# Residual additions, the fourth block difference and two operand splits on VectorE instead of GpSimd, in a two-layer hybrid trunk

## The chip, the cores and the metric

The kernel runs on one core of a Trainium2 chip. The metric is the time of one execution on the device in microseconds (us). The engines go by the profile's names: PE is TensorE (its matmuls), PEld TensorE's weight loads, DVE VectorE, ACT ScalarE, POOL GpSimd, and SP the queue that issues the DMA transfers. Each engine works through a queue of its own in order and waits on semaphores for the others. TensorE's clock is shown as a share of 2.4 GHz, so that 0.50 is its lower level of 1.2 GHz.

## What is computed

An input of 1024 rows by 1024 features goes through two layers, all in float32. In each layer a mixer and a SwiGLU channel mixer (FFN) sit inside a pair of norms with a residual addition:

```python
def rmsnorm(x, g):
    y = x * lax.rsqrt(jnp.mean(x * x, axis=-1, keepdims=True) + RMS_EPS)
    return y * g

def sandwich(x, g_pre, g_post, fn):
    return x + rmsnorm(fn(rmsnorm(x, g_pre)), g_post)

def swiglu(h, w_gate, w_up, w_down):
    return (jax.nn.silu(h @ w_gate) * (h @ w_up)) @ w_down

def even_mixer(t, ...):          # layer 0
    proj = t @ w_in
    y_a = diff_attention(proj[..., :3 * DIFF_WIDTH], ...)
    y_b = conformer_conv(proj[..., 3 * DIFF_WIDTH:], ...)
    return jnp.concatenate([y_a, y_b], axis=-1) @ w_out

def odd_mixer(t, ...):           # layer 1
    proj = t @ w_in
    y_c = s5_ssm(proj[..., :o1], ...)
    y_d = mla_attention(...)
    return jnp.concatenate([y_c, y_d], axis=-1) @ w_out

for layer in (0, 1):
    h = sandwich(h, mix_pre, mix_post, mixer)
    h = sandwich(h, ffn_pre, ffn_post, swiglu)
```

The FFN's inner width is 2816. The state-space layer (s5) needs a few dozen small preparations of its coefficients (exponentials, sines, quotients), each on 128 x 8 numbers.

## The kernel before

**Products.** Each float32 operand of a product is split into a high part (a rounded copy, made by ACT) and a low part (operand minus high part, made by DVE or POOL). A product is then three matmuls (`mm3`, L118 to L120): high by high, high by low, low by high. For the weights of the FFN this is `wsplit`: ACT casts `wh` (L1119), POOL subtracts `wl` (L1121).

**The output projection and its norm.** `w_out_last` runs over eight blocks of 128 rows, once in layer 0 (about 440 to 540 us) and once in layer 1 (about 1610 to 1720 us). Per block it loads a partial sum `pa`, splits the mixer's output into `jt` (high part by ACT L484, low part by DVE L485; one buffer), multiplies it with 4 units of weights in two column halves (24 matmuls into `psw`), and adds each half to `pa` on DVE (L510). Then `sandwich` takes over: the sum of squares on ACT (L106), `rstd` on POOL (L97, L98), the scaling with the post-norm on DVE (L164), the residual addition `nr <- nr + pa` (L165) on the engine that the caller names, a store of `nr`, a second sum of squares and the scaling with the pre-norm on DVE (L169). `nr` has two buffers, `pa` three.

**Into the FFN.** Two blocks later, `Ffn.to_T` transposes the normalised block on TensorE (eight transposes into PSUM `tr`) and cuts it into quarter blocks: `B11`, `B21`, `B22` as high and low parts (L1087, L1088), and four sums or differences kept in `F0` and `F1` (L1080, L1083, L1090, L1091, L1092). The FFN's up projection then follows a one-level fast scheme with seven products instead of eight for each pair of column blocks. `pre` makes the first two products (`b1`, `b2`) of the first pairs between the last blocks of the loop: `c = p + b2` on DVE (L1161) frees the PSUM of `b2`. `x_sums` splits the differences into `T1` to `T4` (L1099 high parts on ACT, L1100 low parts). `pair` makes the products `b5`, `b6`, `b3`, `b7`, `b4` of the differences of weights (`raw`, L1170 and L1171 on DVE) with `T2`, `B22` and so on, and adds them into `p` and `F` on DVE (L1170). `b4` takes the PSUM buffers ("tr") of `b5`, which `F <- p + b5` frees. In layer 0 the small preparations of the state-space layer (`s5_prep`, L525 to L716) lie in the same stretch.

**Order.** The order of the instructions on each engine is not the program's. A scheduler of the framework sorts them, working from its own simulated times; so when an operation is given to another engine, the rows around it, and some far from it, may be sorted otherwise.

Of the kernel before, what the change touches and what calls it, by code (L numbers as in the profile page):

```python
# [10 lines left out]
F32 = mybir.dt.float32  # L11
F32R = mybir.dt.float32r
# [8 lines left out]
P = 128  # L21
S = 1024
D = 1024
HALF = 512
# [11 lines left out]
class Trunk:  # L36
# [134 lines left out]
    def to_T(self, xn, X, b):  # L171
        nc = self.nc
        for q in range(2):
            tr = self.pp.tile([P, 4, P], F32, tag="tr", name="tr")
            for k in range(4):
                d = q * 4 + k
                nc.tensor.transpose(tr[:, k, :], xn[:, d * P:(d + 1) * P], self.ident)
            hi = X[q][:, :, 0, b * P:(b + 1) * P]
            nc.scalar.copy(hi, tr)
            nc.vector.tensor_tensor(X[q][:, :, 1, b * P:(b + 1) * P], tr, hi.bitcast(F32), op=ALU.subtract)  # L180
# [321 lines left out]
    def w_out_last(self, Y, src, res, hout, gpost, gpre, G, pool, fin=None):  # L502
        nc = self.nc
        units = [self.unit(s) for s in src]
        done = []
        for tb in range(8):
            a = pool.tile([P, D], F32, tag="pa", name="pa", bufs=3)
            nc.sync.dma_start(a, self.part[tb * P:(tb + 1) * P, :])
            for cs, ps in self.w_out(Y, units, tb, pool, self.ob, 1):
                nc.vector.tensor_tensor(a[:, cs], ps, a[:, cs], op=ALU.add)  # L510
            self.sandwich(a, tb, res, hout, gpost, gpre, pool.tile([P, D], F32, tag="nr", name="nr", bufs=2), nc.gpsimd)
            done.append(a)
            if tb == 0 and fin is not None:
                fin()
            if tb >= 2:
                G.to_T(done[tb - 2], tb - 2)
            if tb == 6:
                G.pre(0, 0)
        G.pre(0, 1)
        G.to_T(done[6], 6)  # L520
        G.pre(1, 0)
        G.to_T(done[7], 7)
        G.pre(1, 1)
# [528 lines left out]
class Ffn:  # L1052
# [15 lines left out]
    def to_T(self, xn, tb):  # L1068
        K, nc = self.K, self.nc
        t, b = tb // 4, tb % 4  # L1070
        bs = slice(b * P, (b + 1) * P)
        v, sub = nc.vector.tensor_tensor, ALU.subtract
        f0, f1 = [[F[:, q, :, bs] for q in range(2)] for F in (self.F0, self.F1)]
        for q in range(2):
            tr = K.pp.tile([P, 4, P], F32, tag="tr", name="tr")
            for k in range(4):
                d = q * 4 + k
                nc.tensor.transpose(tr[:, k, :], xn[:, d * P:(d + 1) * P], K.ident)
            if t == 0:
                nc.scalar.copy(f0[q], tr)  # L1080
            elif q == 0:
                nc.scalar.copy(f1[0], tr)
                v(f0[0], tr, f0[0], op=sub)  # L1083
            if (q, t) in self.B:
                B = self.B[q, t]
                hi = B[:, :, 0, bs]
                nc.scalar.copy(hi, tr)  # L1087
                v(B[:, :, 1, bs], tr, hi.bitcast(F32), op=sub)  # L1088
        if t:
            v(f1[1], tr, f0[0], op=sub)  # L1090
            v(f1[0], tr, f1[0], op=sub)  # L1091
            nc.gpsimd.tensor_tensor(f0[1], f0[1], f1[1], op=sub)  # L1092

    def x_sums(self, pool):
        nc, K = self.nc, self.K
        F0, F1 = self.F0, self.F1

        def split(T, src, eng):
            nc.scalar.copy(T[:, :, 0, :], src)  # L1099
            eng.tensor_tensor(T[:, :, 1, :], src, T[:, :, 0, :].bitcast(F32), op=ALU.subtract)  # L1100
            return T

        t = lambda n: pool.tile([P, 4, 2, HALF], F32R, tag="tc", name=n, bufs=2)
        self.T1 = split(K.yp.tile([P, 4, 2, HALF], F32R, tag="y", name="T1"), F0[:, 0], nc.vector)
        self.T2 = split(t("T2"), F1[:, 1], nc.vector)
        self.T3 = split(t("T3"), F1[:, 0], nc.gpsimd)
        self.T4 = split(self.bx.tile([P, 4, 2, HALF], F32R, tag="f", name="T4"), F0[:, 1], nc.gpsimd)
        self.E = F0.rearrange("p q (k d) c -> p (q k) d c", d=2)

    def raw(self, src, n=2):  # L1110
# [440 lines left out]
```

## Time and profile before

| | |
|---|---|
| time, median of 3 runs | 2391.94 us (2391.46 to 2400.63) |
| the profiled execution | 2392.32 us, its span 2390.5 us |
| mean granted clock of TensorE | 0.955 |
| TensorE busy | 2172.1 us (91% of the span) |
| VectorE busy | 1587.8 us (66%) |
| ScalarE busy | 952.2 us (40%) |
| GpSimd busy | 1393.1 us (58%) |

"Busy" adds up the time in which an engine has an instruction under way. That includes time in which the instruction is held up by another engine, so a mean duration far above the shortest of the same kind is itself a finding. The chain of work that ended last, which the profile follows back from the end, covers only the last part of the span here; for the stretches around the change the waits of TensorE by line and the timelines are read.

### The profile page before, as it was taken

The numbers are of one execution on the slowest core, as the hardware profiler recorded it, in microseconds if no ns is written. First come the engines' busy times: TensorE is split into PE (matmuls) and PEld (weight loads), VectorE is DVE, ScalarE is ACT, GpSimd is POOL, SyncE is SP. The second block draws the span as 40 slices with busy tenths as digits, with TensorE's granted clock in tenths as the row PEclk, the third lists the DMA queues.
The fourth block names the chain that finished last, engine by engine and source line by source line (L and its number), as shares of the span: only waits on it lengthen the run. The fifth ranks groups of instructions, "written<-read, shape, count | busy, mean of one in ns | idle before, by whom it ended". The sixth has DMA issues, their size and how long they took to land. (4 is left out here: it accounts for less than half of the span.)

```text
span 2390.5 us, 27147 instructions
## 1 busy us (share of the span) xinstructions
PE 2172.1 (91%) x9684; PEld 1755.7 (73%) x9684; DVE 1587.8 (66%) x2091; ACT 952.2 (40%) x1419; POOL 1393.1 (58%) x790
## 2 busy tenths in 40 slices
PE   7999889876999999899768888998799999999995
PEld 5887677665888878688656776876688888877874
DVE  6869567679756865677883467756764444448778
ACT  5554555442222232433243346654522222234332
POOL 5997202264665556787843536423775656569786
PEclk9999899988999999999888999999899999999997
DMA  5134663342332333655453375324432323255543
GB/s 206 62 120 146 172 175 102 107 149 69 121 115 97 125 129 106 198 161 163 125 178 104 110 234 154 115 80 148 138 102 93 127 72 132 75 177 163 164 130 132
DMA packets 153735, 315.34 MB, mean 132 GB/s; under 512 B 20224, under 2 KB 43904, under 8 KB 153600
## 3 DMA queue, kind: packets, MB, share of 16 engines
q1 hardware_dynamic: 153600, 313.60, 40.8%
q8 instruction: 77, 1.26, 0.2%
q14 instruction: 58, 0.48, 0.1%
HBM read 214.39 MB, written 96.01 MB: 130 GB/s over the span
## 5 line engine op out<-in xcount | busy, mean ns | idle before, releaser
L1121 POOL TENSOR_TENSOR wl<-raw,wh 128x1024 fp32r<-128x1024 f32 (+1 forms) x238 | 607.4, 2556 | 335.9 <-ACT wh L1119 319.4
L1119 ACT CAST wh<-raw 128x1024 fp32r<-128x1024 f32 (+1 forms) x238 | 242.7, 1023 | 456.8 <-PE b L119 258.9
L118 PE MATMUL b<-T,wh 128*128 128x512 f32 x704 | 277.9, 396 | 16.3 <-DVE F L1170 13.0
L120 PE MATMUL b<-T,wl 128*128 128x512 f32 x704 | 277.4, 394 | 1.1 <-POOL wl L1121 1.1
L119 PE MATMUL b<-T,wh 128*128 128x512 f32 x704 | 277.7, 394 | 0.6 <-DVE T L1100 0.6
L118 PE MATMUL psd<-wh,hh 128*128 128x512 f32 x552 | 222.8, 404 | 37.7 <-DVE acc L1229 26.5
L118 PE MATMUL b<-B,wh 128*128 128x512 f32 x528 | 209.2, 397 | 21.2 <-DVE c L1161 17.6
L119 PE MATMUL psd<-wl,hh 128*128 128x512 f32 x552 | 219.9, 398 | 0.0
L120 PE MATMUL psd<-wh,hl 128*128 128x512 f32 x552 | 219.1, 398 | 0.0
L119 PE MATMUL b<-B,wh 128*128 128x512 f32 x528 | 208.2, 395 | 0.7 <-DVE B L1088 0.7
L120 PE MATMUL b<-B,wl 128*128 128x512 f32 x528 | 207.7, 395 | 0.8 <-POOL wl L1121 0.8
L1229 DVE TENSOR_TENSOR acc<-acc,psd 128x1024 f32<-128x1024 f32 x124 | 150.7, 1217 | 82.7 <-PE psd L120 82.6
L1170 DVE TENSOR_TENSOR p<-p,b 128x1024 f32<-128x1024 f32 (+1 forms) x88 | 83.4, 949 | 144.6 <-PE b L120 134.7
L1248 ACT CAST hh<-hr 128x1024 fp32r<-128x1024 f32 (+1 forms) x84 | 82.4, 981 | 240.0 <-PE psd L119 215.1
L118 PEld LDWEIGHTS b<-T,wh 128*128 128x128 f32 x704 | 133.1, 189 | 47.8 <-issue 13.6
L118 PEld LDWEIGHTS psd<-wh,hh 128*128 128x128 f32 x552 | 106.1, 192 | 70.1 <-issue 27.9
L91 POOL TENSOR_TENSOR wl<-raw,wh 128x1024 fp32r<-128x1024 f32 x48 | 121.6, 2546 | 61.6 <-ACT wh L89 61.4
L120 PEld LDWEIGHTS b<-T,wl 128*128 128x128 f32 x704 | 133.1, 189 | 31.8 <-POOL wl L1121 1.5
L119 PEld LDWEIGHTS b<-T,wh 128*128 128x128 f32 x704 | 133.3, 189 | 31.0 <-DVE T L1100 1.1
L1249 DVE TENSOR_TENSOR hl<-hr,hh 128x1024 fp32r<-128x1024 f32 (+1 forms) x84 | 145.7, 1738 | 11.9 <-ACT hh L1248 11.9
L1273 POOL TENSOR_TENSOR raw<-raw 128x1024 f32<-128x1024 f32 (+1 forms) x50 | 123.4, 2468 | 20.7 <-DMA raw<-in_l_dn_dram 18.3
L1171 DVE TENSOR_TENSOR raw<-raw 128x1024 f32<-128x1024 f32 x66 | 108.3, 1640 | 40.4 <-POOL wl L1121 39.1
(420 smaller groups left out, 5209.2 us busy)
## 6 DMA issues: line engine op xcount, KB each, us to landing
raw<-in_l_gu_dram SPq DMA_DIRECT2D x96, 512.0 KB, 3.5
hr<-l_h_s SPq DMA_DIRECT2D x70, 512.0 KB, 3.9
raw<-in_l_dn_dram SPq DMA_DIRECT2D x48, 512.0 KB, 3.8
l_h_s<-F SPq DMA_DIRECT2D x66, 256.0 KB, 2.2
raw<-in_w_in_dram SPq DMA_DIRECT2D x27, 512.0 KB, 4.0
l_h_s<-c SPq DMA_DIRECT2D x44, 256.0 KB, 2.0
l_h_s<-p SPq DMA_DIRECT2D x44, 256.0 KB, 2.4
raw<-in_l_w_out_dram SPq DMA_DIRECT2D x16, 512.0 KB, 4.1
```

Source lines behind the costliest of these rows:

```text
L91: nc.gpsimd.tensor_tensor(lo, raw, hi.bitcast(F32), op=ALU.subtract)
L118: mm(ps, ah, bh, start=first, stop=False)
L119: mm(ps, ah, bl, start=False, stop=False)
L120: mm(ps, al, bh, start=False, stop=last)
L1119: nc.scalar.copy(hi[:, 0:n], r[:, 0:n])
L1121: nc.gpsimd.tensor_tensor(lo[:, 0:n], r[:, 0:n], hi[:, 0:n].bitcast(F32), op=ALU.subtract)
L1170: add = lambda o, a, b: v.tensor_tensor(o, a, b, op=ALU.add)
L1171: sub = lambda o, a, b: v.tensor_tensor(o, a, b, op=ALU.subtract)
L1229: add = lambda o, a, b: v.tensor_tensor(o, a, b, op=ALU.add)
L1248: nc.scalar.copy(hi[:, 0:n], r[:, 0:n])
L1249: v.tensor_tensor(lo[:, 0:n], r[:, 0:n], hi[:, 0:n].bitcast(F32), op=ALU.subtract)
L1273: g = lambda o, x, y: nc.gpsimd.tensor_tensor(o[:, s], x[:, s], y[:, s], op=ALU.subtract)
```

## The change

Three edits give operations from POOL to DVE. The residual additions of `w_out_last` (L165, 16 of 128x1024, eight per layer) go to DVE; the additions at the end of the FFNs (which have other callers) stay where they are. The fourth block difference in `to_T` (L1092, 8 of 128x512) goes to DVE. The low parts of `T3` and `T4` in `x_sums` (L1100, 4 of 128x2048, two per layer) go to DVE.

```diff
@@ w_out_last
             for cs, ps in self.w_out(Y, units, tb, pool, self.ob, 1):
                 nc.vector.tensor_tensor(a[:, cs], ps, a[:, cs], op=ALU.add)
-            self.sandwich(a, tb, res, hout, gpost, gpre, pool.tile([P, D], F32, tag="nr", name="nr", bufs=2), nc.gpsimd)
+            self.sandwich(a, tb, res, hout, gpost, gpre, pool.tile([P, D], F32, tag="nr", name="nr", bufs=2), nc.vector)
             done.append(a)
@@ Ffn.to_T
             v(f1[1], tr, f0[0], op=sub)
             v(f1[0], tr, f1[0], op=sub)
-            nc.gpsimd.tensor_tensor(f0[1], f0[1], f1[1], op=sub)
+            v(f0[1], f0[1], f1[1], op=sub)
@@ Ffn.x_sums
         self.T1 = split(K.yp.tile([P, 4, 2, HALF], F32R, tag="y", name="T1"), F0[:, 0], nc.vector)
         self.T2 = split(t("T2"), F1[:, 1], nc.vector)
-        self.T3 = split(t("T3"), F1[:, 0], nc.gpsimd)
-        self.T4 = split(self.bx.tile([P, 4, 2, HALF], F32R, tag="f", name="T4"), F0[:, 1], nc.gpsimd)
+        self.T3 = split(t("T3"), F1[:, 0], nc.vector)
+        self.T4 = split(self.bx.tile([P, 4, 2, HALF], F32R, tag="f", name="T4"), F0[:, 1], nc.vector)
```

The scheduler sorts the queues anew. Three places are shown, all on DVE; the number behind a name is that of its buffer.

The first is one block of the loop in layer 0: the block whose sum is `pa_4136` and whose split is `jt_4205`. Before:

```order
L510 TENSOR_TENSOR pa_4136<-psw_4141,pa_4136 128x512
L169 SCALAR_TENSOR_TENSOR pa_4002<-nr_4035,rstd_4049,gpre_3874 128x1024
L164 SCALAR_TENSOR_TENSOR pa_4069<-pa_4069,rstd_4107,gpost_3872 128x1024
L510 TENSOR_TENSOR pa_4136<-psw_4155,pa_4136 128x512
L485 TENSOR_TENSOR jt_4205<-yattn_2337,jt_4205 128x4x128
L1088 TENSOR_TENSOR B11_3864<-tr_4187,B11_3864 128x4x128
L1088 TENSOR_TENSOR B21_3865<-tr_4195,B21_3865 128x4x128
```

Now:

```order
L510 TENSOR_TENSOR pa_4136<-psw_4141,pa_4136 128x512
L510 TENSOR_TENSOR pa_4136<-psw_4155,pa_4136 128x512
L169 SCALAR_TENSOR_TENSOR pa_4069<-nr_4102,rstd_4116,gpre_3874 128x1024
L485 TENSOR_TENSOR jt_4205<-yattn_2337,jt_4205 128x4x128
L164 SCALAR_TENSOR_TENSOR pa_4136<-pa_4136,rstd_4174,gpost_3872 128x1024
L1088 TENSOR_TENSOR B11_3864<-tr_4254,B11_3864 128x4x128
L165 TENSOR_TENSOR nr_4169<-nr_4169,pa_4136 128x1024
L1088 TENSOR_TENSOR B21_3865<-tr_4262,B21_3865 128x4x128
```

The residual addition L165 stands between the two `B` splits. The two norm scalings have moved by a block: L164 now belongs to the block whose projection has just ended (`pa_4136`, before it was the one ahead of it), L169 to the block ahead of that, and the transposed block comes one block earlier.

The second is the tail of the loop in layer 0: `c11` are the sums that free `b2`, `raw` the weight sums of the first pair. Before:

```order
L1170 TENSOR_TENSOR raw_4612<-raw_4608,raw_4610 128x1024
L1171 TENSOR_TENSOR raw_4608<-raw_4604,raw_4608 128x1024
L169 SCALAR_TENSOR_TENSOR pa_4270<-nr_4303,rstd_4317,gpre_3874 128x1024
L164 SCALAR_TENSOR_TENSOR pa_4371<-pa_4371,rstd_4409,gpost_3872 128x1024
L1171 TENSOR_TENSOR raw_4612<-raw_4612,raw_4604 128x1024
L1083 TENSOR_TENSOR F0_3868<-tr_4478,F0_3868 128x4x128
L1088 TENSOR_TENSOR B22_3866<-tr_4485,B22_3866 128x4x128
L1171 TENSOR_TENSOR raw_4606<-raw_4606,raw_4612 128x1024
L1090 TENSOR_TENSOR F1_3867<-tr_4485,F0_3868 128x4x128
L1091 TENSOR_TENSOR F1_3867<-tr_4485,F1_3867 128x4x128
L1161 TENSOR_TENSOR c11_4471<-p1_4369,b2_4445 128x512
L1161 TENSOR_TENSOR c11_4472<-p1_4369,b2_4446 128x512
```

Now:

```order
L169 SCALAR_TENSOR_TENSOR pa_4270<-nr_4303,rstd_4317,gpre_3874 128x1024
L1170 TENSOR_TENSOR raw_4612<-raw_4608,raw_4610 128x1024
L164 SCALAR_TENSOR_TENSOR pa_4371<-pa_4371,rstd_4409,gpost_3872 128x1024
L1171 TENSOR_TENSOR raw_4608<-raw_4604,raw_4608 128x1024
L165 TENSOR_TENSOR nr_4404<-nr_4404,pa_4371 128x1024
L1171 TENSOR_TENSOR raw_4612<-raw_4612,raw_4604 128x1024
L1161 TENSOR_TENSOR c11_4471<-p1_4369,b2_4445 128x512
L1161 TENSOR_TENSOR c11_4472<-p1_4369,b2_4446 128x512
```

The residual addition of the last block stands ahead of `c11`; the quarter-block operations of the block before (L1083 to L1091) and one weight difference (`raw_4606`) now stand behind it.

The third is the start of the pairs in layer 0. Before, the low parts of `T1` and `T2` are followed by 97 rows, nearly all of them small ones of `s5_prep` (`xd` is one of its tiles), and only then by the additions of the first pair. Its first rows before:

```order
L1100 TENSOR_TENSOR T1_4592<-F0_3868,T1_4592 128x4x512
L544 TENSOR_SCALAR xd1_5313<-xd1_5313 128x8
L1100 TENSOR_TENSOR T2_4595<-F1_3867,T2_4595 128x4x512
L545 SCALAR_TENSOR_TENSOR xd2_5314<-xd1_5313,xd0_5312 128x8
L546 SCALAR_TENSOR_TENSOR xd2_5314<-xd1_5313,xd2_5314 128x8
L547 TENSOR_SCALAR xd3_5315<-xd2_5314 128x8
```

Now `T3` follows `T2` after one small row, `T4` after eight more, and the additions of the pair begin seven rows behind `T4`:

```order
L1100 TENSOR_TENSOR T4_4601<-F0_3868,T4_4601 128x4x512
L593 COPY dt_5311<-xd3_5315 128x8
L596 TENSOR_TENSOR x_5438<-lam_5303,dt_5311 128x8
L542 TENSOR_SCALAR xm0_5441<-x_5438 128x8
L543 TENSOR_SCALAR xm1_5442<-xm0_5441 128x8
L601 TENSOR_SCALAR x_5438<-x_5438 128x8
L544 TENSOR_SCALAR xm1_5442<-xm1_5442 128x8
L1170 TENSOR_TENSOR raw_4798<-raw_4794,raw_4796 128x1024
L545 SCALAR_TENSOR_TENSOR xm2_5443<-xm1_5442,xm0_5441 128x8
L1170 TENSOR_TENSOR p1_4369<-p1_4369,b6_4645 128x1024
L1171 TENSOR_TENSOR raw_4794<-raw_4790,raw_4794 128x1024
```

The addition `F0 <- p1 + b5`, on which `b4` waits, stands three rows further on, and some 80 small rows that stood ahead of it now stand behind it, among the pairs that follow.

## Rows read from the trace of the kernel before

**Rows 1.** The page's first part: busy us of each engine (share of span) xinstructions.

```profile
PE 2172.1 (91%) x9684; PEld 1755.7 (73%) x9684; DVE 1587.8 (66%) x2091; ACT 952.2 (40%) x1419; POOL 1393.1 (58%) x790
```

**Rows 2.** Waits of PE, 440 to 620 us: line, releaser: us in total, times, longest.

```profile
PE b L118 <- DVE F L1170: 13.0, 1, 13.0
PE b L118 <- DVE c L1161: 8.5, 1, 8.5
PE psw L120 <- DVE jt L485: 3.6, 3, 1.7
PE psw L118 <- ACT jt L484: 3.0, 3, 1.4
PE b L118 <- ACT wh L1119: 2.5, 1, 2.5
```

**Rows 3.** Waits of PE, 1610 to 1790 us.

```profile
PE b L118 <- DVE c L1161: 9.1, 1, 9.1
PE psw L120 <- DVE jt L485: 5.1, 4, 1.7
```

**Rows 4.** POOL's groups (busy us, mean ns), then DVE's by line (ns min/median/max, starts).

```profile
L165 POOL TENSOR_TENSOR nr<-nr,pa 128x1024 f32<-128x1024 f32 x16 | 40.0, 2501 | 39.1 <-DVE pa L164 37.7 <-PE psw L120 1.5
L1100 POOL TENSOR_TENSOR T<-F,T 128x2048 fp32r<-128x2048 f32 x4 | 20.7, 5163 | 10.9 <-ACT T L1099 10.9
L1092 POOL TENSOR_TENSOR F<-F,F 128x512 f32<-128x512 f32 x8 | 10.8, 1351 | 1.1 <-DVE F L1090 0.8
...
L165 DVE TENSOR_TENSOR acc<-acc,acc x12: 1207/1224/2771, 1209.6 to 2385.1; 128x1024 f32<-128x1024 f32 x12
...
L1100 DVE TENSOR_TENSOR T<-F,T x4: 2273/2276/2279, 552.0 to 1738.5; 128x2048 fp32r<-128x2048 f32 x4
```

**Rows 5.** Timeline, block loop, layer 0 (start us, us; [idle before]); last, all of L485.

```profile
482.93 1.28 DVE L164 SCALAR_TENSOR_TENSOR pa<-pa,rstd,gpost 128x1024 f32<-128x1024 f32 x1
...
484.72 2.49 DVE L485 TENSOR_TENSOR jt<-yattn,jt 128x512 fp32r<-128x512 f32 x1
...
484.28 2.38 POOL L165 TENSOR_TENSOR nr<-nr,pa 128x1024 f32<-128x1024 f32 x1 [3.26 <-DVE pa L164]
...
487.26 0.51 PE L120 MATMUL psw<-wh,jt 128*128 128x512 f32 x1 [1.67 <-DVE jt L485]
...
L485 DVE TENSOR_TENSOR jt<-yattn,jt x16: 683/1834/2508, 447.1 to 1681.8; 128x512 fp32r<-128x512 f32 x16
```

**Rows 6.** Stretches: length, busy us (instructions) by engine, then PE's clock, DMA share, GB/s.

```profile
487.30:491.00 3.70, 3.70 (x10) 2.91 (x11) 1.11 (x2) 1.59 (x4) 1.47 (x4) 0.55 0.45 175
584.40:589.60 5.20, 5.20 (x12) 4.09 (x13) 5.20 (x7) 0.36 (x1) 2.54 (x1) 0.50 0.00 0
600.00:620.00 20.00, 20.00 (x88) 16.23 (x87) 19.86 (x16) 4.73 (x5) 13.25 (x7) 0.99 0.54 165
```

**Rows 7.** Timelines of DVE and of POOL, tail of the loop in layer 0.

```profile
528.98 3.37 DVE L164 SCALAR_TENSOR_TENSOR pa<-pa,rstd,gpost 128x1024 f32<-128x1024 f32 x1
...
534.61 2.18 DVE L1171 TENSOR_TENSOR raw<-raw 128x1024 f32<-128x1024 f32 x1
...
532.43 3.27 POOL L165 TENSOR_TENSOR nr<-nr,pa 128x1024 f32<-128x1024 f32 x1 [1.16 <-DVE pa L164]
535.66 3.34 POOL L1121 TENSOR_TENSOR wl<-raw,wh 128x1024 fp32r<-128x1024 f32 x1
```

**Rows 8.** Timeline of DVE, T stage of layer 0, 556 to 585 us.

```profile
556.47 4.64 DVE L545 SCALAR_TENSOR_TENSOR xd<-xd,xd 128x8 f32<-128x8 f32 x1
561.15 2.33 DVE L546 SCALAR_TENSOR_TENSOR xd<-xd,xd 128x8 f32<-128x8 f32 x1
563.52 4.53 DVE L547 TENSOR_SCALAR xd<-xd 128x8 f32<-128x8 f32 x1
...
572.93 0.16 DVE L570 TENSOR_TENSOR cs<-cs 128x8 f32<-128x8 f32 x1
...
583.55 1.27 DVE L1170 TENSOR_TENSOR F<-p,b 128x512 f32<-128x512 f32 x2
...
```

## Prediction, made before the changed kernel was run

> **What bounds the kernel now.** I read the page first, then TensorE's waits, then the timelines around the longest of them. The page's busy line says TensorE (PE) is busy for 91% of the span, with VectorE (DVE) at 1587.8 us and GpSimd (POOL) at 1393.1 us [rows 1]. So a change on DVE and POOL is worth only what it takes from TensorE's idle stretches and from the slow clock behind them. Nearly all code that the diff touches lies in two stretches: the output projection of layer 0 and the start of its FFN (about 440 to 620 us), and the same in layer 1 (about 1610 to 1790 us). In the first, TensorE loses 13.0 us to the wait for `F` (L1170), 8.5 us to `c` (L1161), 3.6 us in three pieces to `jt` (L485) and 3.0 us in three to ACT's half of `jt`; 2.5 us go to a cast of `wh` [rows 2]. In the second, `c` costs 9.1 us and `jt` 5.1 us in four pieces; no wait for `F` stands there [rows 3]. From 600 us on TensorE is busy in all 20 us of a 20 us window [rows 6], so time won before that point is not handed to another wait at once.
>
> Each of these waits has the same pattern behind it. In the block loop POOL begins an addition `nr` at 484.28 us; DVE's lo half of `jt`, which starts 0.44 us later, takes 2.49 us where the shortest of the same line takes 0.683 us, and TensorE idles 1.67 us for it [rows 5]. So a DVE operation that reads two operands and starts while a POOL addition runs ends about when that addition does. In the tail of the loop, L164 takes 3.37 us and L1171 2.18 us in the same way, where undisturbed ones take 1.28 and some 1.22 us [rows 4, 5, 7]; both stand ahead of the `c` additions that TensorE waits for. In the T stage three operations on 128x8 elements take 4.64, 2.33 and 4.53 us, where one of their kind takes 0.16 us [rows 8]; POOL's two T splits of layer 0 run beside them, at 5.16 us each on average [rows 4].
>
> A wait also costs clock. Behind the wait at 487 us ten matmuls fill 3.70 us at a granted clock of 0.55, and behind the one at 584 us twelve fill 5.20 us at 0.50, against 88 in 20.00 us at 0.99 [rows 6]. At 20.00/88 = 0.227 us a matmul, this is 1.4 and 2.5 us lost beside the idle time itself.
>
> **The change part by part.**
>
> Work that moves. POOL loses 16 additions of 2.50 us (40 us), 8 of 1.35 us (11 us) and 4 splits of 5.16 us (21 us). DVE gains 16 at 1.22 us (19.6 us, by the additions of the same shape that it already does), 8 at about half of that (an estimate, half as wide: 4.9 us) and 4 at 2.27 us (9.1 us) [rows 4]. POOL's 72 us and DVE's 34 us lie beside other work, so their sums cost nothing by themselves; what counts is the place in the queue.
>
> (1) The block loops. The row of `nr` moves into DVE's queue, behind L485 and L164 of its block as the order shows, so L485 can no longer be held by it. The 3.6 us of layer 0 go, and at least the one slow stretch of 1.4 us: 5.0 us. In layer 1 I take the 5.1 us of four waits and no clock: 5 us. The cover is DVE's own time: a block holds 24 matmuls, 24 x 0.227 = 5.4 us, and eight transposes, and DVE's seven operations in it are, by the nearest rows, two 128x1024 scalings of 1.28 us, one addition of 1.22 us and four 128x512 of about 0.68 us [rows 4, 5, 7], 6.5 us in sum. That is tight: what is late next is ACT's half of `jt` (3.0 us stay in the sum) or DVE itself. Ends: nothing (if L485 stands behind L169 and L164 for as long as it was held), or 3.6 + 5.1 + 7 x 1.4 = 18 us. I take 10, since one slow stretch of three is on a row.
>
> (2) The tails, `c` in each layer. DVE's L164 comes down from 3.37 us to some 1.28 (2.1 us), and L1171 from 2.18 us to 1.22 (1.0 us); the addition itself, 1.22 us, now stands ahead of `c` on DVE. Net 1.9 us. POOL, free of an addition of 3.27 us and of a fourth difference of 1.35 us, can make the next `wl` earlier [rows 4, 7]: at most 4.6 us more. So between a loss of 1 us (nothing held any longer than now, the addition added) and a gain of 6 us; I take 4 in each layer, 8 in all. What is late next is the same `c`, some 4 us.
>
> (3) The T stage of layer 0. From the end of T2's split (556.5 us) to the `F` additions (583.55 us) DVE takes 27 us, of which 11.5 are the three held operations and the rest 94 small ones of the state-space preparation [rows 8]. In the new order T3 and T4 (2 x 2.27 = 4.5 us), some 16 small ones (2.6 us) and three additions of 1.22 us stand there: 10.8 us, so `F` could be freed at about 567 us. TensorE ran out of work 13.0 us before the wait's end at 584.4, at 571.4 [rows 2, 6]. By that the whole 13.0 us go; I take 10, leaving room for one or two holds of 2 us by POOL's `wl` that still run there. With the wait goes the slow stretch, 2.5 us [rows 6], and the wait for `wh` (2.5 us [rows 2]), whose `raw` sum stands in the same DVE queue. Sum 15 us. Ends: 5 us (if three holds of about 2 us and the small operations stay ahead) and 18 us. In layer 1 no TensorE wait for `F` is on the page, and T3 and T4 there are worth nothing.
>
> (4) The rest. The final additions of layer 1 stay with POOL; the rest of the program is only re-sorted by a few rows, and I count it at nothing, within 5 us either way, more than the 2.5 us of the `wh` wait and less than the sum of two such.
>
> By the profile the shared hold works both ways: a POOL addition of 2.50 us becomes a DVE one of 1.22 us, which can hold POOL for half as long [rows 4]. The Trainium skill speaks against the change here: *Perfetto Trace Analysis*, section "Optimizing Scalar/DVE Operations", says that GpSimd and DVE share an SBUF read port, so that moving operations between the two might not help. By that sentence nothing would be gained and the time would stay near 2392 us; the trace agrees on the sharing, but shows DVE to be twice as fast at the same operation.
>
> **The rivals.**
>
> - *Everything comes in.* 18 + 11 + 18 = 47 us: 2345 us. For it: each hold is on a row and its cause leaves the queue. Against: POOL's `wl` (3.34 us in the tail [rows 7]) goes on holding DVE.
> - *Only the loops gain.* In the tails and the T stage DVE's longer queue takes the place of the holds: the additions, T3 and T4 are 1.22 and 2 x 2.27 us of in-order work ahead of `c` and `F`, and `wl` still blocks. Then 10 us remain: 2382 us. This is where the shared-port argument would lead as a mechanism of this kernel. For it: DVE is busy for 19.86 of 20 us right behind the stage [rows 6]. Against: TensorE's 13.0 us of idle time is more than the 4.5 us that are added.
> - *DVE becomes the bound of the first FFN pairs: slower.* The order puts some 80 small state-space operations behind the `F` additions, among the pairs that follow, where TensorE has no idle time. They are 80 x 0.16 = 13 us undisturbed; one in four held for 2 us, as L164 is [rows 7], makes 40 us more. With DVE at 19.86 of 20 us [rows 6], they would be TensorE's wait: 2392 - 33 + 53 = 2412 us. It decides from 45 us of such waits on (2404 - 2359). Against: DVE has room in later pairs, and only what frees a PSUM buffer stops TensorE.
>
> **How the numbers follow.** The profiled execution took 2392.32 us against a median of 2391.94, so the sum stands for both. 10 + 8 + 15 = 33 us less: 2359 us, between 2347 and 2375 by the ends of the terms taken singly. Chances: forecast 0.59, everything 0.18, only the loops 0.15, slower 0.08. A measurement of this kernel tells about 0.5% (12 us) from no change, so the bounds are 2380 and 2404. Faster takes the first two, and a third of the third: 0.81; same is the rest of the third and the near side of the last: 0.12; slower 0.07. The range goes from 2340 (everything, and 5 us of re-sorting) to 2382.
>
> **What would show it.** Right: the `jt` waits of L485 near zero and its median near 0.69 us; `c` waits of about 4 us; the `F` wait under 3 us, with no stretch at half clock behind it; about 28 more DVE operations and POOL's busy time down by some 70 us. The first rival shows L164 or L165 on DVE held by `wl` and the `F` wait still above 8 us. The slower one shows new waits of TensorE for L1170 between 600 and 700 us behind rows of 128x8. I am wrong if TensorE's waits in the two stretches go and the span doesn't shorten: then the gain was given back in a part that I count at nothing.

## The result

The changed kernel takes 2360.12 us (median of 4 runs, 2357.66 to 2364.36) against 2391.7 us (median of 4 runs, 2388.27 to 2400.63) for the kernel before: a ratio of 0.986, with a 95% interval of 0.9835 to 0.9886, or 32 us. The forecast was 2359 us, within 2340 to 2382.

The first lines of the page after, which answer to [rows 1] (busy us, share of the span, instructions):

```profile
span 2359.2 us, 27146 instructions
...
PE 2167.2 (92%) x9684; PEld 1751.7 (74%) x9684; DVE 1598.5 (68%) x2119; ACT 953.0 (40%) x1419; POOL 1329.8 (56%) x762
```

DVE has 28 operations more and is busy for only 10.7 us more, though [rows 4] price what it took over at 34 us: by that difference some 23 us of its busy time before was time in which POOL held it (an estimate, net of the new holds shown below). POOL is busy 63 us less, not the 72 us that it gave away, since its other operations take a little longer now (`wl` 2.68 us on average, before 2.63).

TensorE's waits after, first in layer 0 (440 to 640 us), then in layer 1 (1590 to 1770 us); line, releaser: us in total, times, longest. They answer to [rows 2, 3]:

```profile
PE b L118 <- DVE c L1161: 4.0, 1, 4.0
PE b L120 <- POOL wl L1121: 3.9, 2, 3.5
PE psw L118 <- ACT jt L484: 3.5, 5, 1.3
PE b L118 <- DVE F L1170: 1.7, 1, 1.7
PE psw L118 <- DVE pa L510: 1.5, 2, 0.8
...
PE b L118 <- DVE c L1161: 4.5, 1, 4.5
PE psw L118 <- ACT jt L484: 3.2, 3, 1.3
PE b L118 <- ACT B L1087: 3.1, 1, 3.1
PE b L119 <- DVE B L1088: 2.3, 1, 2.3
PE b L118 <- DVE pa L510: 1.9, 1, 1.9
```

The waits for L485 are gone from both stretches, `F` is down from 13.0 to 1.7 us, `c` from 8.5 and 9.1 to 4.0 and 4.5. New or longer are the waits for `wl` (3.5 us) in layer 0, for `B` (3.1 and 2.3 us) in layer 1, and for DVE's additions L510 (1.5 and 1.9 us), which now stand behind others in its queue.

L485 in the two loops and the lines moved (ns min/median/max, first and last start), and three stretches (length, busy us of PE, PEld, DVE, ACT, POOL, then PE's clock, DMA share, GB/s). They answer to [rows 4 to 6]:

```profile
L485 DVE TENSOR_TENSOR jt<-yattn,jt x16: 678/685/693, 448.1 to 1649.8; 128x512 fp32r<-128x512 f32 x16
L165 DVE TENSOR_TENSOR nr<-nr,pa x16: 1209/1215/3384, 459.0 to 1675.8; 128x1024 f32<-128x1024 f32 x16
L1092 DVE TENSOR_TENSOR F<-F,F x8: 673/691/2274, 508.1 to 1694.8; 128x512 f32<-128x512 f32 x8
L1100 DVE TENSOR_TENSOR T<-F,T x8: 2272/2275/2292, 540.7 to 1705.1; 128x2048 fp32r<-128x2048 f32 x8
...
487.30:491.00 3.70, 3.70 (x21) 3.16 (x21) 3.00 (x4) 2.06 (x4) 0.94 (x2) 1.00 0.74 219
563.90:569.00 5.10, 5.08 (x23) 4.24 (x23) 5.10 (x12) 1.69 (x2) 1.45 (x1) 1.00 0.29 84
601.80:607.60 5.80, 5.76 (x14) 4.50 (x15) 5.80 (x8) 0.00 (x0) 3.35 (x2) 0.50 0.11 36
```

L485 is never held in the two loops (0.69 us at most). The moved operations take what was forecast at their median, and can be held themselves: L165 for 3.38 us at worst, L1092 for 2.27. The first two stretches run at full clock; the third, behind the new wait for `wl`, at half clock.

**Where the time went** is read best from one and the same matmul in both traces. The table gives its start before and after, and what was won or lost since the row above (the shift is after minus before):

| event on TensorE | before | after | shift | since the row above |
|---|---|---|---|---|
| first matmul of the projection's last part, layer 0 | 447.12 | 448.13 | +1.0 | |
| its last matmul (end of the loop) | 515.44 | 510.55 | -4.9 | -5.9 loop |
| first product with a `T` (end of the tail) | 554.56 | 545.41 | -9.2 | -4.3 tail |
| 337th FFN matmul into `b` | 625.64 | 597.62 | -28.0 | -18.9 T stage |
| 481st FFN matmul into `b` | 658.62 | 637.92 | -20.7 | +7.3 given back |
| first matmul of the down projection | 985.25 | 964.84 | -20.4 | +0.3 |
| its last, layer 0 | 1197.14 | 1174.51 | -22.6 | -2.2 |
| first matmul of the scan, layer 1 | 1318.52 | 1291.94 | -26.6 | -4.0 |
| last product of the attention, layer 1 | 1624.61 | 1597.66 | -27.0 | -0.4 |
| last matmul of the projection, layer 1 | 1691.86 | 1659.13 | -32.7 | -5.8 loop |
| first product with a `T`, layer 1 | 1734.02 | 1701.71 | -32.3 | +0.4 tail |
| last matmul of the program | 2378.84 | 2347.54 | -31.3 | +1.0 |

### The profile page after: what moved, and what is told of

Its sections match the earlier page's. It is cut to its first block, busy times and chain, and to the rows that moved or that the text cites. A ratio compares the mean times of both kernels' runs of the same rounds, so it can differ in the third digit from the quotient of the medians.

```text
span 2359.2 us, 27146 instructions
## 1 busy us (share of the span) xinstructions
PE 2167.2 (92%) x9684; PEld 1751.7 (74%) x9684; DVE 1598.5 (68%) x2119; ACT 953.0 (40%) x1419; POOL 1329.8 (56%) x762
## 4 chain that ended last, share of the span: by engine, by line
PE 70%; DVE 13%; DMA 5%; POOL 5%; issue 4%; ACT 3%; SPq 0%; POOLq 0%; ACTq 0%; DVEq 0%
PE b L120 10%; PE b L119 10%; PE b L118 10%; PE psd L118 5%; PE psd L119 4%; PE psd L120 4%; PE psw L118 2%; PE psw L120 2%; PE psw L119 2%; PE psc L118 2%; PE psc L119 2%; PE pss L1036 2%; PE psc L120 2%; POOL wl L1121 1%; PE trp L361 1%
## 5 line engine op out<-in xcount | busy, mean ns | idle before, releaser
L1121 POOL TENSOR_TENSOR wl<-raw,wh 128x1024 fp32r<-128x1024 f32 (+1 forms) x238 | 617.9, 2600 | 358.2 <-ACT wh L1119 351.3
L118 PE MATMUL b<-B,wh 128*128 128x512 f32 x528 | 211.5, 401 | 14.6 <-DVE c L1161 8.5
L119 PE MATMUL b<-B,wh 128*128 128x512 f32 x528 | 210.9, 399 | 3.2 <-DVE B L1088 3.2
L1171 DVE TENSOR_TENSOR raw<-raw 128x1024 f32<-128x1024 f32 x66 | 107.8, 1633 | 42.7 <-POOL wl L1121 41.5
```

The costliest lines, as they stand in the source:

```text
L118: mm(ps, ah, bh, start=first, stop=False)
L119: mm(ps, ah, bl, start=False, stop=False)
L1121: nc.gpsimd.tensor_tensor(lo[:, 0:n], r[:, 0:n], hi[:, 0:n].bitcast(F32), op=ALU.subtract)
L1171: sub = lambda o, a, b: v.tensor_tensor(o, a, b, op=ALU.subtract)
```

## The experiments

Besides the changed kernel, eleven were run. The three edits are called R (residual additions, L165), D (fourth difference, L1092) and S (the splits of T3 and T4). A fourth edit, "late", makes the small state-space operations wait for a pair of the FFN: their first tile is first written from `F`, so its load, and all behind it, has to wait.

| kernel | ratio to before (95%) | loop 0 | tail 0 | T stage | loop 1 | tail 1 |
|---|---|---|---|---|---|---|
| changed (R, D, S) | 0.986 (0.9835-0.9886) | -5.9 | -4.3 | -11.5 | -5.8 | +0.4 |
| R | 0.9923 (0.9907-0.9939) | -5.9 | +1.2 | -5.0 | -6.0 | -1.7 |
| S | 0.996 (0.9942-0.9978) | -1.6 | +1.8 | -10.6 | -1.5 | +0.5 |
| D | 0.9983 (0.9967-0.9998) | 0.0 | +0.8 | -1.6 | -1.5 | -2.7 |
| R, S | 0.9902 (0.9873-0.9932) | -4.3 | +0.7 | -11.9 | -6.2 | -1.2 |
| R, D | 0.9912 (0.9889-0.9935) | -5.9 | -5.9 | -2.2 | -6.1 | -2.2 |
| late alone | 0.9923 (0.9908-0.9939) | -1.6 | +2.2 | -19.6 | -1.5 | +0.4 |
| R, D, S, late | 0.9862 (0.9831-0.9892) | -5.9 | -3.8 | -20.1 | -5.5 | -0.1 |
| R, S, late | 0.9875 (0.9845-0.9906) | -5.9 | +2.0 | -21.4 | -6.0 | -1.4 |
| R, D, late | 0.9859 (0.9842-0.9876) | -5.9 | -3.9 | -19.9 | -6.0 | -1.4 |
| R, D, S, later (pair six) | 0.9894 (0.9876-0.9913) | -5.9 | -4.0 | -20.1 | -6.1 | -1.6 |

The five columns are changes of stretches of the table above in us (T stage: from the first product with a `T` to the 481st matmul into `b`), each from one trace. Stretches that an edit doesn't touch vary by up to 2.2 us in these traces, so that much is noise of one trace or of the new sorting. The kernel with halved additions has its numbers in the text below.

**R alone.**

```diff
-            self.sandwich(a, ..., name="nr", bufs=2), nc.gpsimd)
+            self.sandwich(a, ..., name="nr", bufs=2), nc.vector)
```

> The 16 residual additions (L165) alone go to DVE; the fourth difference and the T3/T4 splits stay on POOL. Theory (each part pays at its own place): the L485 waits of TensorE go from 3.6 and 5.1 us to under 1 each, both loops end about 6 us earlier relative to their start, the c waits fall to about 5 us, and the F wait of layer 0 stays at 10 to 13 us, since the order still has the 94 small state-space operations ahead of F. Time about 2392 - 12 - 5 = 2375 us (2370 to 2380). Rival (the sorting of the whole program is what paid): the loops gain no more than 3 us each and the time stays above 2382.

Measured: 2370.61 us against 2389.64 (ratio 0.9923). L485 takes 0.693 us at most, both loops are 6 us shorter, as in the changed kernel. The waits of TensorE in layer 0 (440 to 640 us), columns as above:

```profile
PE b L118 <- DVE F L1170: 7.0, 2, 6.7
PE b L118 <- DVE c L1161: 4.2, 1, 4.2
...
PE b L119 <- DVE B L1088: 2.1, 1, 2.1
PE b L118 <- ACT B L1087: 1.6, 1, 1.6
```

`c` is down to 4.2 us there, but the tail as a whole isn't shorter: the waits for `B` behind it are longer (2.1 and 1.6 us). In layer 1 `c` stays at 9.2 us. `F` came down to 6.7 us, though 10 to 13 were expected. So the loops belong to R; the tails do not by R alone. The time is at the lower end of what was expected.

**S alone, and D alone.**

```diff
-        self.T3 = split(t("T3"), F1[:, 0], nc.gpsimd)
-        self.T4 = split(self.bx.tile(...), F0[:, 1], nc.gpsimd)
+        self.T3 = split(t("T3"), F1[:, 0], nc.vector)
+        self.T4 = split(self.bx.tile(...), F0[:, 1], nc.vector)
```

> The low parts of T3 and T4 alone go to DVE. Theory: the loops stay as before (L485 waits 3.6 and 5.1 us), the c waits stay at 8 to 9 us, the F wait of layer 0 falls under 3 us, and a new wait for wl appears in the second pair, as in the changed kernel, since the small operations stand behind F in this order too. Net of the T stage -12 us: about 2380 us (2376 to 2385). Rival (without the other two parts DVE reaches the stage too late): F wait above 8 us and 2388 to 2394.

Measured: 2381.7 us (ratio 0.996). The `F` wait is 4.0 us, not under 3, the L485 waits stay at 3.6 and 5.2 us, the `c` waits at 8.5 and 9.1, and a wait for `wl` of 2.4 us appears. The T stage is 10.6 us shorter, nearly as in the changed kernel. In this order 47 small operations still stand between T2's split and the `F` additions, 105 before and 21 in the changed kernel.

```diff
-            nc.gpsimd.tensor_tensor(f0[1], f0[1], f1[1], op=sub)
+            v(f0[1], f0[1], f1[1], op=sub)
```

> The fourth block difference (L1092) alone goes to DVE. Theory: nothing waits for it, the F wait and the L485 waits stay, the c waits change by less than 2 us: 2388 to 2394 us. Rival (it shortens POOL's queue ahead of wl and so the c wait by 3 us or more in each layer): below 2386.

Measured: 2386.29 us (ratio 0.9983, interval up to 0.9998), a little below the forecast stretch; `c` stays at 8.5 and 9.8 us, so the rival's mechanism is not there. The three edits alone come to 19.0 + 7.9 + 3.4 = 30.3 us by their medians, nearly the 32 us of all three.

**What sets the `F` wait: the kernel before with the small operations late.**

```diff
-    def s5_prep(self, pool):
+    def s5_prep(self, pool, G):
...
-        lam = sm("lam", (P, 3, 8))
+        lam = sm("lam", (P, 3, 8)); v.tensor_copy(lam[:, 0, :], G.F0[:, 0, 0, 0:8])
...
-        G.up(lambda: K.s5_prep(p5))
+        G.up(lambda: K.s5_prep(p5, G))
```

> The kernel before with one edit: the preparation of the state-space layer is made to wait for the third pair of layer 0 (its first tile is first written from F, a copy of 128x8, then overwritten by its load). All splits and additions stay on their engines of before. Two theories of the F wait of 13.0 us in layer 0. Small operations ahead of F: with them gone the F wait falls under 3 us though T3 and T4 still run on POOL, and the time to 2392 - 19 = 2373 us or a little more. T splits on POOL as such: b7 and b4 wait for T3 and T4 on POOL (4.6 us each, one behind the other, with wl between them) and TensorE still loses 8 us or more there: 2382 to 2392.

Measured: 2371.24 us (ratio 0.9923): with no operation of the change, the time is 18 us shorter. The T stage alone is 19.6 us shorter in its trace, with no wait for `F` in it; the shifts of the other stretches add up to about nothing. Timelines of this kernel, DVE and then POOL (start us, us; [idle before <- releaser]):

```profile
554.55 2.27 DVE L1100 TENSOR_TENSOR T<-F,T 128x2048 fp32r<-128x2048 f32 x1
568.40 1.22 DVE L1170 TENSOR_TENSOR p<-p,b 128x1024 f32<-128x1024 f32 x1 [11.58 <-PE b L120]
569.66 1.28 DVE L1170 TENSOR_TENSOR F<-p,b 128x512 f32<-128x512 f32 x2
...
555.40 5.99 POOL L1100 TENSOR_TENSOR T<-F,T 128x2048 fp32r<-128x2048 f32 x1 [3.05 <-ACT T L1099]
563.69 4.63 POOL L1100 TENSOR_TENSOR T<-F,T 128x2048 fp32r<-128x2048 f32 x1
```

The two splits on POOL take about as long as before (5.99 and 4.63 us), and DVE is idle for 11.6 us until TensorE brings its product: with no small operations there, the splits delay nobody. What delayed `F` before was the queue of small operations ahead of it, with its held ones: POOL's splits and the `wl` between them made three of them long [rows 8], and a fourth, L549 at 573.91 us, took 2.31 us beside a `wl`. These four fill 13.8 of the 27.0 us between T2's split and `F`, two sums 2.4 us and the other small ones the remaining 10.8 us.

**The changed kernel with the small operations late, and the same without S.**

> The changed kernel with the preparation of the state-space layer made to wait for the third pair of layer 0. Theory (the small operations among the pairs cause the new wait for wl in the second pair, 3.5 us, and the half clock behind it): both go, and the time is about 7 us shorter than the changed kernel's, 2353 us (2350 to 2356). Rival: the same operations hold up later pairs just as much, and the time stays at 2358 to 2362.

Measured: 2357.71 us (2355.38 to 2357.97; ratio 0.9862). The wait for `wl` falls from 3.5 to 1.0 us, the T stage is 20.1 us shorter, so what the changed kernel gives back is kept. But the time is only 2.4 us below the changed kernel's, inside the spread of both: by the trace, 3.5 us go again in later pairs, where the small operations now are (from 635 us on). So the time lies between the two forecasts: the wait for `wl` goes, as the theory has it, and later pairs pay for part of it, as the rival has it. The timeline of TensorE there shows the wait for `F`:

```profile
671.14 0.47 PE L118 MATMUL b<-T,wh 128*128 128x512 f32 x1 [1.76 <-DVE F L1170]
```

Then R and D with the small operations in their place, T3 and T4 split on POOL:

> The residual additions and the fourth difference on DVE, T3 and T4 on POOL as before. In this order the small state-space operations stand ahead of F again. Theory (what stands ahead of F on DVE sets the T stage): an F wait of 5 to 8 us as with the residual additions alone, the first two thirds of the gain elsewhere kept: 2366 to 2371 us. Rival (the T stage takes its gain from an earlier start, with the splits anywhere): F wait under 3 us and 2358 to 2363.

Measured: 2370.1 us (ratio 0.9912), with an `F` wait of 9.4 us, more than the 5 to 8 expected, though the time is as forecast: with the small operations ahead of `F` and the splits on POOL the T stage gains 2.2 us only. One of the 82 small operations there is held behind four operations of POOL in a row, the two splits and two `wl`, and ends with the last of them (DVE, then the first of POOL's):

```profile
545.51 13.93 DVE L545 SCALAR_TENSOR_TENSOR xd<-xd,xd 128x8 f32<-128x8 f32 x1
...
543.53 6.65 POOL L1100 TENSOR_TENSOR T<-F,T 128x2048 fp32r<-128x2048 f32 x1 [5.25 <-DMA T_s<-pz]
```

The same with "late":

> As the last one, with the preparation of the state-space layer made to wait for the third pair. Theory (with the small operations away, it makes no difference on which engine T3 and T4 are split): no F wait over 2 us at the start of the pairs, and the time within 3 us of the changed kernel with the same wait (2358 us). Rival (POOL's splits of 4.6 us delay b7, b4 or wl): 2363 us or more, with a wait for T or wl of over 3 us at the start of the pairs.

Measured: 2357.74 us (2355.48 to 2359.37; ratio 0.9859), 0.03 us from the kernel with S. Once the small operations are away, it makes no measurable difference on which engine T3 and T4 are split. With the small operations in place S does two things at once: it takes away the holds by the splits, and the sorting puts many of the small operations behind `F`. No run has the splits on DVE with all the small operations still ahead of `F`, so what each of the two is worth by itself was not measured.

**The place of the small operations.**

```diff
-                if i == 3 and mid is not None:
+                if i == 6 and mid is not None:
```

> The changed kernel with the preparation of the state-space layer made to wait for the sixth pair instead of the third. If the 3.5 us that the third-pair version gives back (a wait for F of 1.8 us and slow clock) come from one unlucky meeting, they go: about 2354 us. If the small operations cost about that wherever they land: 2356 to 2359 us, with a wait for F among pairs six to eight.

Measured: 2364.98 us (ratio 0.9894), worse than either forecast. The wait for `F` of 1.75 us is there again, at 748.5 us, so the first theory falls. The trace loses 3.5 us within the pairs, as with the third pair, and 7.4 us more at the start of the down projection, where TensorE's wait for `hh` is 12.1 us in place of the kernel before's 5.4. Which row makes that wait longer was not followed up.

**D in the tails.**

> The changed kernel with the fourth block difference back on POOL. Theory (L1092 on DVE, held 2.24 us by wl between two c additions in the tail of layer 1, is what gave back the shorter c wait there): the waits for B in that tail, 3.1 and 2.3 us, fall under 2 us together and the time is 2354 to 2358. Rival (wl would hold another operation of DVE in its place): 2358 to 2364.

Measured: 2365.61 us (ratio 0.9902), above both forecasts: not faster than the changed kernel but, by the trace's stretches, 5 us slower in the tail of layer 0 (+0.7 against -4.3). In layer 1 the waits for `B` do fall (to 1.0 us), but `c` is back at 9.2 us. The tail of layer 1 differs by 1.6 us (-1.2 against +0.4), which is within the noise of two traces, so the theory that D spoils it isn't borne out.

> Both edits together: the fourth block difference back on POOL, and the preparation of the state-space layer late. If both theories hold, the gains add: 2348 to 2351 us. If the difference's place doesn't matter, as after_late: 2350 to 2356.

Measured: 2359.27 us (2356.03 to 2366.61; ratio 0.9875), outside both forecasts. The T stage gains 21.4 us, the tail of layer 0 nothing (+2.0): the two theories don't add.

**Half of each addition on either engine.**

```diff
-        eng.tensor_tensor(r, r, acc, op=ALU.add)
+        [e.tensor_tensor(r[:, k], r[:, k], acc[:, k], op=ALU.add) for k, e in enumerate(eng)] ...
```

> The kernel before with each of the 16 residual additions cut in two: POOL adds the first 512 columns, DVE the second. Theory (a DVE operation of two operands that starts under a POOL addition ends with it): POOL's part takes about 1.3 us, so the longest L485 falls from 2.5 us to about 1.4 to 1.6, and the L485 waits of TensorE fall to a third or less of 3.6 and 5.1 us; the time is between that of before and that with the additions on DVE alone, 2375 to 2385 us. Rival (the hold isn't tied to the length of POOL's operation): L485 still reaches 2.3 us or more.

Measured: 2371.73 us (2367.60 to 2381.64; ratio 0.9932, interval 0.9907 to 0.9957). L485 takes 0.693 us at most, so it isn't held for half as long, it isn't held at all; the waits for it fall from 5.1 to 1.5 us in layer 1 and vanish in layer 0. The time is below the forecast stretch. (The trace is of an execution of 2381.35 us, 10 us above the median; 6.7 us of that are lost ahead of the loop of layer 0.) The timeline (POOL, then DVE) shows why the run doesn't settle the question that it was made for:

```profile
481.78 1.29 POOL L165 TENSOR_TENSOR nr<-nr,pa 128x512 f32<-128x512 f32 x1 [1.40 <-DVE pa L164]
...
482.22 0.68 DVE L510 TENSOR_TENSOR pa<-psw,pa 128x512 f32<-128x512 f32 x1
483.42 0.68 DVE L165 TENSOR_TENSOR nr<-nr,pa 128x512 f32<-128x512 f32 x1
484.03 0.69 DVE L510 TENSOR_TENSOR pa<-psw,pa 128x512 f32<-128x512 f32 x1
484.68 0.69 DVE L485 TENSOR_TENSOR jt<-yattn,jt 128x512 fp32r<-128x512 f32 x1
```

POOL's shorter half is over before DVE comes to L485, so neither the theory nor its rival is tested. One thing it does show: L510, which reads one operand from PSUM and one from SBUF, starts 0.44 us into POOL's addition and still takes 0.68 us. In the kernel before, L510 at 484.12 us, beside POOL's addition of 484.28 us, took 0.68 us too, while L485, with both operands in SBUF, was held [rows 5]. By the Trainium skill, *SBUF — State Buffer*, section "Who interferes with whom", a DVE instruction with two SBUF inputs contends with a GpSimd instruction that reads SBUF, and one with at most one SBUF input does not, outside the modes in which copies, casts and `tensor_scalar` take both ports. These rows agree, with the exception too: L547, a `TENSOR_SCALAR` of one operand, took 4.53 us in the kernel before [rows 8].

## Why the prediction was right, step by step

The time came out 1 us from the forecast. That the sum fits so well is luck: the loops and the tail of layer 0 came near their terms, the tail of layer 1 and the T stage fell short, and a part that was counted at nothing paid.

**(1) The loops: right.** 10 us were forecast, 5.9 and 5.8 came. R alone gives 5.9 and 6.0, and without R no kernel gives over 1.6 except the halved additions. The cause is the one named: in these loops L485 is never held in any kernel with R. The clock over the loops rises from 0.95 and 0.97 to 1.00. What was late next is ACT's half of `jt`, as said (3.5 and 3.2 us), and in layer 0 DVE itself with L510 (1.5 us).

**(2) The tails: right in size in layer 0, wrong in layer 1.** Four us each were forecast. In layer 0 4.3 came; but neither R (+1.2) nor D (+0.8) gives it alone, R and D together do (-5.9). The step that failed in both layers is "L164 comes down from 3.37 us" as a gain: POOL's addition did not hold L164. Beside it ran `wl`, which stays on POOL, and in the changed kernel a `wl` holds the next one in the queue, in layer 0 the addition itself (before, then after; in layer 1 it is L1171, for 3.40 us):

```profile
533.41 0.68 DVE L1083 TENSOR_TENSOR F<-tr,F 128x512 f32<-128x512 f32 x1
...
528.21 3.05 POOL L1121 TENSOR_TENSOR wl<-raw,wh 128x1024 fp32r<-128x1024 f32 x1
...
522.54 3.38 DVE L165 TENSOR_TENSOR nr<-nr,pa 128x1024 f32<-128x1024 f32 x1
...
521.46 3.38 POOL L1121 TENSOR_TENSOR wl<-raw,wh 128x1024 fp32r<-128x1024 f32 x1 [3.12 <-ACT wh L1119]
```

What shortened the `c` wait is, by the rows, the new order, which puts the quarter-block operations (L1083 to L1091) and one `raw` behind `c`. In layer 0 they filled DVE from 533.41 us to the start of `c` at 537.90 us, 4.5 us, and the wait fell by 4.5 us. In the other kernels it goes the same way: with these operations behind `c` the wait is 4.0 to 5.1 us, with them (or some of them) ahead of it 8.5 to 9.8 us, as in layer 1 of R alone. Only the kernel with halved additions doesn't follow this (8.6 and 7.0 us; several operations ahead of `c` are held there). No run changed the order alone.

In layer 1 the `c` wait fell by 4.6 us, as forecast, and the tail didn't become shorter. DVE there (start us, us), POOL, and TensorE's next waits:

```profile
1658.85 3.22 DVE L165 TENSOR_TENSOR nr<-nr,pa 128x1024 f32<-128x1024 f32 x1
...
1685.05 1.85 DVE L1143 TENSOR_TENSOR c<-c,c 128x512 f32<-128x512 f32 x1
1686.83 0.67 DVE L1161 TENSOR_TENSOR c<-p,b 128x512 f32<-128x512 f32 x1
1687.43 2.24 DVE L1092 TENSOR_TENSOR F<-F,F 128x512 f32<-128x512 f32 x1
1689.60 0.67 DVE L1161 TENSOR_TENSOR c<-p,b 128x512 f32<-128x512 f32 x1
1690.37 2.06 DVE L1143 TENSOR_TENSOR c<-c,c 128x512 f32<-128x512 f32 x1
...
1683.95 7.93 POOL L1121 TENSOR_TENSOR wl<-raw,wh 128x1024 fp32r<-128x1024 f32 x3 [2.30 <-ACT wh L1119]
...
1690.19 1.22 PE L118 MATMUL b<-B,wh 128*128 128x512 f32 x2 [3.14 <-ACT B L1087]
1693.69 0.80 PE L119 MATMUL b<-B,wh 128*128 128x512 f32 x1 [2.28 <-DVE B L1088]
```

The second pair of `c` additions is cut in two by L1092, now on DVE and held by three `wl` of POOL in a row; L1143 is held on either side of it. On ACT the last block's `B` stands behind the first of these `c`, on DVE behind L1092 and the second L1143, and TensorE waits 5.4 us there, where 2.4 us stood before, with half clock behind it. Another 1.9 us go to L510 at the start of the tail, which stands behind the addition, held for 3.22 us beside a `wl`; before, no wait for L510 stood there. Together, -4.6 + 3.0 + 1.9 = +0.3 us, and +0.4 was measured. So "what is late next is the same `c`" failed too: late next was the step behind it, and the addition on DVE was itself held.

**(3) The T stage: the mechanism right, the terms off.** 15 us were forecast between 5 and 18; 11.5 came. It is 18.9 us won and 7.3 given back. The first part beat the best case: TensorE waits 1.7 us for `F`, the clock stays up behind it (1.00 in the stretch from 563.9 us), and the wait for `wh` is gone. The forecast put 10.8 us between T2's split and the `F` additions, with one or two holds beside that. It was 17.3 us in place of 27.0: three small operations are still held, now by `wl` alone, for 7.1 us together,

```profile
548.06 2.38 DVE L546 SCALAR_TENSOR_TENSOR xd<-xd,xd 128x8 f32<-128x8 f32 x1
...
554.17 2.36 DVE L593 COPY dt<-xd 128x8 f32<-128x8 f32 x1
...
560.77 2.34 DVE L546 SCALAR_TENSOR_TENSOR xm<-xm,xm 128x8 f32<-128x8 f32 x1
```

T3 and T4 take 4.6 us, three sums 3.7 us and the other small ones 2.0 us. So the holds give 13.8 - 7.1 = 6.7 us, and the order gives 10.8 - 2.0 = 8.8 us on the small operations and takes 4.6 + 1.2 for the splits and one more sum. Both were in the forecast's sum; its 11.5 us of holds missed the fourth one, and that `wl` would go on holding was priced too low. The small operations are needed for this wait (late alone -19.6 us; R, D and late -19.9, with the splits on POOL). How much the splits' engine gives with the small operations in place is read from these rows and was not run.

What was given back is the slower rival, in small. It was priced at 53 us, if a quarter of the small operations among the pairs were held. The rows around the new wait, DVE, ACT, POOL and TensorE of the changed kernel:

```profile
582.17 2.38 DVE L598 COPY mag<-xm 128x8 f32<-128x8 f32 x1
...
584.55 2.36 DVE L570 TENSOR_TENSOR cs<-cs 128x8 f32<-128x8 f32 x1
...
595.29 0.68 DVE L1170 TENSOR_TENSOR F<-F,b 128x512 f32<-128x512 f32 x1
...
596.00 0.63 ACT L1142 ACTIVATE F<-F 128x512 f32<-128x512 f32 x1 [13.01 <-DVE F L1170]
596.54 1.98 ACT L1119 CAST wh<-raw 128x1024 fp32r<-128x1024 f32 x2
...
597.65 4.13 POOL L1121 TENSOR_TENSOR wl<-raw,wh 128x1024 fp32r<-128x1024 f32 x1 [3.27 <-ACT wh L1119]
...
601.84 0.79 PE L120 MATMUL b<-B,wl 128*128 128x512 f32 x1 [3.48 <-POOL wl L1121]
```

Small operations keep the `F` addition until 595.3 us. From 577 us to that point DVE is busy for all but 0.04 us, and five of them are held: the two shown for 2.4 us each, three others for 1.3 us each. ACT's activation waits for that addition, the casts of `wh` stand behind that on ACT, POOL's `wl` behind the casts, itself held to 4.13 us, and TensorE behind `wl`. The wait is 3.5 us; at half clock 14 matmuls in 5.80 us lose another 5.80 - 14 x 0.227 = 2.6 us. So the mechanism was there and its size was a seventh of the price (7.3 of 53 us): five holds, not twenty, stood ahead of that addition. The other small operations cost less than was priced, too: undisturbed, one often starts 0.08 us after the one before it, though each takes 0.16 us (in the kernel before L549 at 571.13, L552 at 571.21 and L558 at 571.28 us).

**(4) The rest: counted at nothing, within 5 us either way.** 1.0 us was lost ahead of the loops, 2.2 won in the down projection and 4.0 around the norm of layer 1 (between 1197 and 1319 us before), 1.0 lost at the end. The 4 us stand on no operation of the diff: the traces with R alone and with D alone show them too (-3.7 and -3.8), those with S alone and with R and D don't (+0.1 and -0.3). Which of the re-sorted rows there decides it was not tried and stays open.

So the sum came out at 33 against 31 because errors cancelled: 7.9 us less in the T stage (3.5) and in layer 1's tail (4.4), 2 us more in the loops and in layer 0's tail, and 4.3 us more outside the change. The prediction's own span "by the ends of the terms taken singly", 2347 to 2375, doesn't follow from its terms: one term at its end gives 2351 to 2369.

**The rule against the change.** That moving operations between GpSimd and DVE might not help, as the Trainium skill has it (*Perfetto Trace Analysis*, "Optimizing Scalar/DVE Operations"), doesn't hold for R, which is worth 19 us alone. For S the engine made no difference once the small operations were away (2357.71 against 2357.74 us); with them in place it was not measured apart from the order.

**A kernel faster than both?** R, D and late (2357.74 us) and R, D, S and late (2357.71) have the lowest medians, 2.4 us below the changed kernel, which is inside the spread of the runs. No kernel here is shown to beat it.

## What to carry to other kernels

Look first at what stands ahead of the wanted operation in its queue, and only then at what makes the queue slow: taking a queue of a hundred small operations out of the way was worth 18 us, and once they were away it made no difference on which engine the splits that had held them ran. When an operation is given to another engine under a scheduler that sorts, read the new order at the waits, since the sorting can carry more of the gain than the operation does; and where work is moved behind a wait, name the next wait that it can cause. A forecast that hits the time can still have its terms wrong: compare the start of the same matmul in both traces, stretch by stretch.

## What the runs showed that was not expected

- An engine's busy time is no measure of its work where two engines hold each other: DVE took over 34 us of operations and was busy 10.7 us longer.
- Small operations cost about the same wherever they were placed among the pairs: 3.5 us, with a wait for `F` of 1.76 us behind the third pair and of 1.75 us behind the sixth. With the later place the start of the down projection was late as well (a wait of 12.1 us in place of 5.4).
- One operation on 128x8 numbers was held for 13.93 us, behind four POOL operations that followed each other without a gap (R and D).
- An operation with one operand in PSUM was not held by a POOL addition that ran beside it (L510, 0.68 us), where one with both operands in SBUF was (L485, 2.49 us).
